# First layer's modulation weights in 256-column pieces, with three pairs of output tiles beside them

## The chip, the cores and the metric

The kernel runs on one core of one Trainium2 chip. The metric is device time in microseconds (us), the median of the runs; before the change it is 2983.74 us (three runs, 2981.06 to 2984.47). Engines are called as the profile calls them: PE (matrix products), PEld (its weight loads), DVE (vector), ACT (scalar), POOL (GpSimd) and SP (which here only issues transfers from HBM).

## The reference

Two transformer blocks run one after the other on 256 tokens of width 2048; everything is float32. The change is in the first layer of the first block, before its attention:

```
silu_c, silu_cc = silu(c), silu(c_ctx)
for l in range(2):
    shift, scale, gate       = split(silu_c  @ w_mod[l] + b_mod[l], 3)     # w_mod[l]: 2048 x 6144
    shift_c, scale_c, gate_c = split(silu_cc @ w_mod[l] + b_mod[l], 3)
    n  = rms_norm(h,  g[l]) * (1 + scale)   + shift        # 256 latent tokens
    nc = rms_norm(hc, g[l]) * (1 + scale_c) + shift_c      # 256 context tokens
    p, pc = split(n @ w_in[l]), split(nc @ w_in[l])        # w_in[l]: 2048 x 7168
    ... four kinds of attention on p, pc; gate; @ w_out[l]; rms_norm; residual ...
```

The second block (a state-space mixer, a latent attention and a feed-forward part) is not touched.

## The kernel before

Activations lie transposed: 16 chunks of 128 features by 512 tokens (256 latent, 256 context). `hb` holds the input, `nH` and `nL` the normed input as a high and a low part, so that three matmuls in a reduced format make one float32 product. Weights of w_in come as a stream of units: one unit is four chunks by 256 output columns, 512 KB, in one of three tiles `raw` (class `Stream`, `RB = 3`). ACT casts a unit to `wh`, DVE subtracts to get `wl`, and only that subtraction frees the `raw` tile for the load of the unit three places later. `W.take` emits cast and subtraction; `W.load_to` emits loads. All instructions are emitted in a fixed order by hand: each engine runs its own in the order in which the code emits them, and SP's loads too, so a load that waits for a tile holds back every load behind it.

The start of layer 0 works like this. `first_norm` squares and sums `hb`, makes the reciprocal root `rb` and multiplies chunks of `hb` by it (`times_rb`, four chunks at a time). Meanwhile `mod_load` brings w_mod in pieces of 512 columns (16 chunks of 256 KB) into 22 slots of 256 KB, and `mod_first` multiplies a piece by silu(c) on PE: four blocks of four matmuls (L706), each of the four on 32 of PE's columns, all in float32. The result is copied out by ACT (`row`), transposed by four tiny matmuls (L717, tile X) and added to the bias (L718). Pieces 4 to 7 are the scale, 0 to 3 the shift; once both pieces for four chunks are there, `gains` makes the factor `gsc`, `norm_in` norms four chunks, and the products of the first two output pairs (`DUO`, the value columns of head group A) over these four chunks run between the blocks of the next two pieces (`first_steps`). The last four chunks of DUO run after the last piece. Then `layer_in` takes one output pair after another, four units each: first the key columns `("k","A",0)`, then the query columns `("q","A",0)`, and so on. Beside each step of `layer_in` run steps of the gate's w_mod pieces and of layer 1's (`mod_later`).

A value pair's products are matmuls with 256 moving columns (L370 to L372), those of the other pairs have 512 (L464 to L466).

Of the kernel before, what the change touches and what calls it, by code (L numbers as in the profile page):

```python
# [19 lines left out]
D = 2048  # L20
# [11 lines left out]
def _r(a, b):  # L32
    return np.arange(a, b)
# [179 lines left out]
def _layout(i):  # L213
    g = {}
    x, ctx = i["x"][0], i["ctx"][0]
    g["xc"] = np.concatenate([_xt(x), _xt(ctx)], axis=2)
    g["cT"] = np.ascontiguousarray(np.stack([i["c"][0].reshape(16, 128).T, i["c_ctx"].reshape(16, 128).T], axis=2))
    for l in range(2):
        units = []
        for key, cols in WIN:  # L220
            units += _pack(i["w_in"][l], 4, cols)
        g[f"win{l}"] = np.concatenate(units)
        g[f"wmod{l}"] = np.concatenate([u for q in range(12) for u in _pack(i["w_mod"][l], 1, _r(512 * q, 512 * q + 512))])
        g[f"wout{l}"] = np.concatenate([u for q in range(8) for u in _pack(i["w_out"][l], 4, _r(256 * q, 256 * q + 256))])
# [20 lines left out]
def program(ctx: ExitStack, tc: tile.TileContext, A, stop=None):  # L245
# [368 lines left out]


    FULL, LATC, CTXC = (0, 512), (0, 256), (256, 512)
    DUO, TRIO = ORDER[0][:2], ORDER[1][:3]
    for l in range(2):
        for part in ("c", "")[1 - l:]:
            for j in range(4):  # L620
                for i in (DUO, TRIO)[l]:
                    W.add((l, *part) + WIN[i][0], f"win{l}", 4 * i + j, 1)
        for i in ORDER[l][3 if l else 2:]:
            W.add((l,) + WIN[i][0], f"win{l}", 4 * i, 4)
        for m in range(8 if l else 5):
# [36 lines left out]
    V.memset(csq, 0.0)  # L662
    V.tensor_copy(out=csq[:, :, 0:2], in_=cs)

    def mod_acc(acc, v, k, w, first):
        if first:
            V.tensor_scalar(acc, w, cs[:, k, v:v + 1], None, op0=MUL)
        else:
            V.scalar_tensor_tensor(out=acc, in0=w, scalar=cs[:, k, v:v + 1], in1=acc, op0=MUL, op1=ADD)  # L669

    def mod_src(l, q, k, n):
        off = (q * 16 + k) * 65536
        return A[f"wmod{l}"][off:off + n * 65536].rearrange("(k p m) -> p k m", p=128, k=n)

    def slots():
# [5 lines left out]

    slot = slots()

    def mod_load(q):

        out = [next(slot) for _ in range(16)]
        k = 0
        while k < 16:
            t, j = out[k]
            n = 1  # L690
            while k + n < 16 and n < 4 and out[k + n][0] is t:
                n += 1
            SY.dma_start(out=t[:, j:j + n, :], in_=mod_src(0, q, k, n))
            k += n
        return [t[:, j, :] for t, j in out]

    fins = []

    def mod_first(q, steps):

        raw = mod_load(q)
        ps = ps_("S")
        for k0 in range(0, 16, 4):

            for j in range(4):
                T.matmul(ps[32 * j:32 * j + 32, :], csq[:, k0 + j, :], raw[k0 + j], start=(k0 == 0), stop=(k0 == 12))  # L706
            if k0 == 0 and fins:
                fins.pop(0)()
            for _ in range(2 if k0 == 0 else 4):
                next(steps, None)  # L710
        row = aw.tile([128, 512], F32, tag=("sqa", "ptl")[q // 4], name="row", bufs=1)
        S.copy(out=row, in_=ps)

        def finish():
            pt = ps_("X")
            for j in range(4):
                T.matmul(pt[:, 2 * j:2 * j + 2], row[:, j * 128:(j + 1) * 128], sel, start=True, stop=True)  # L717
            V.tensor_tensor(out=mod[0][:, :, 4 * q:4 * q + 4].rearrange("p v j -> p j v"),  # L718
                            in0=pt[:, :8].rearrange("p (j v) -> p j v", v=2),
                            in1=bmod[:, 0, 4 * q:4 * q + 4].unsqueeze(2).to_broadcast([128, 4, 2]), op=ADD)  # L720
            if q < 4:
                gains(0, 4 * q, 4 * q + 4)
        fins.append(finish)

    def mod_later(l, q, vs):
# [56 lines left out]
                         scale=gsc[:, v, k:k + 1], bias=mod[0][:, v, k:k + 1])  # L782
        split(nH[:, k, :], nL[:, k, :], t)

    duo_ps = [[ps_(t) for t in tags] for tags in (("mm", "mm"), ("mm", "PT"))]

    def times_rb(j, eng):
        for k in range(4 * j, 4 * j + 4):
            eng.tensor_tensor(out=hb[:, k, 2:514], in0=hb[:, k, 2:514], in1=rb, op=MUL)

    def prod_of(i):
        return products_v if WIN[i][0][0] == "v" else products

    def first_steps(j):

        ws = []
        for i in DUO:
            ws.append(W.take((0,) + WIN[i][0], 256, False))
            yield
        for k in range(4):  # L800
            norm_in(4 * j + k)
            yield
        if j < 3:
            times_rb(j + 1, V)
        for i in range(4):
            for ps, w, prods in zip(duo_ps, ws, map(prod_of, DUO)):
                prods(ps, w[i:i + 1], N_, (FULL, FULL), 4 * j + i, KC, lambda t, k: t[:, k, :])
                for _ in range(2):
                    yield

    for k in range(4):
        SY.dma_start(out=hb[:, 4 * k:4 * k + 4, 2:514], in_=A["xc"][:, 4 * k:4 * k + 4, :])
# [2 lines left out]
    def first_norm():  # L815
# [10 lines left out]
                yield  # L826
        V.tensor_tensor(out=xacc, in0=xacc, in1=xacc2, op=ADD)
        yield
        yield from rstd_row("O", [xacc], 512, D, rb)
        yield  # L830
        times_rb(0, V)

    steps = first_norm()
    for _ in range(4):
        next(steps)
    mod_first(4, steps)
    mod_first(0, steps)
    run_now(steps)
    W.load_to(2)
    for j in range(3):  # L840
        steps = first_steps(j)
        mod_first(5 + j, steps)
        mod_first(1 + j, steps)
        run_now(steps)
        W.load_to(2 * j + 4)
    fins.pop(0)()
    run_now(first_steps(3))

    def dump_split(h, lo, dst):
        o = t2k("dbg")  # L850
        V.tensor_tensor(out=o[:, :h.shape[1]], in0=h.bitcast(F32), in1=lo.bitcast(F32), op=ADD)
# [2 lines left out]
    if stop == "n0":  # L854
# [1 line left out]
            dump_split(nH[:, k, :], nL[:, k, :], A["dbg"][:, k, :])  # L856
        b1.close()
        return


    lamc = const.tile([128, 2, 2], F32, name="lamc")
    lamt, pr = p2k("lamt"), p2k("lamp")
    lamt = lamt.rearrange("p (l i d) -> p l i d", l=2, i=4)
    pr = pr[:, :256].rearrange("p (l i d) -> p l i d", l=2, i=2)
    S.dma_start(out=lamt, in_=A["lam"])
    V.tensor_tensor(out=pr, in0=lamt[:, :, 0::2, :], in1=lamt[:, :, 1::2, :], op=MUL)
    sm4 = small("lam4", 4, 1)
    sm4v = sm4.rearrange("p (l i) -> p l i", i=2)
    V.tensor_reduce(out=sm4v, in_=pr, axis=AX.X, op=ADD)
    S.activation(out=sm4, in_=sm4, func=AF.Exp)  # L870
    for l in range(2):
        li = 0.8 - 0.6 * math.exp(-0.3 * l)

        V.tensor_tensor(out=lamc[:, l, 0:1], in0=sm4v[:, l, 1:2], in1=sm4v[:, l, 0:1], op=SUB)
        V.tensor_scalar(lamc[:, l, 0:1], lamc[:, l, 0:1], li, None, op0=SUB)

        V.tensor_scalar(lamc[:, l, 1:2], subg[:, l:l + 1], 0.5 * (1.0 - li), None, op0=MUL)


    def horner(q, x, cs_, first):  # L880
# [543 lines left out]
        return lambda ps: evac_qk(l, key[0], key[1], key[2], ps, rg[0], n, new)  # L1424

    def layer_in(l):
        for i in ORDER[l][3 if l else 2:]:
            key = WIN[i][0]
            rg = FULL if l == 0 or key[0] in "kv" else LATC
            if l:  # L1430
                beside["rate"] = RATE["long"] if rg == FULL else RATE["short"]
            pair((l,) + key, rg, in_evac(l, key, rg), prods=prod_of(i))

    def layer_in3(part, rg, before, new):

        keys = [WIN[i][0] for i in TRIO]
        trio([(1, *part) + key for key in keys], rg, [in_evac(1, key, rg, new) for key in keys], before, [prod_of(i) for i in TRIO])

    tails = []
    accs, acc_of = (lambda: p2k("zacc"), lambda: acc272[:, 16:]), [None]  # L1440
# [101 lines left out]
        vp.add(mod_later(1, q, (0, 1)))  # L1542
    for q in range(8, 12):
        vp.add(mod_later(1, q, (0,)))
    for i, ps in zip(DUO, duo_ps):
        pend.append(lambda ps=ps, f=in_evac(0, WIN[i][0], FULL): f(ps))
    layer_in(0)
    if stop == "att0":
        drain(pipe, vp)
# [770 lines left out]
```

## Time and profile before

| what | value |
|---|---|
| median of 3 runs | 2983.74 us |
| profiled execution | 2980.39 us, span 2978.6 us |
| PE busy | 2798.6 us, 94% |
| DVE, ACT, POOL busy | 66%, 43%, 18% |
| HBM traffic in the first 117 us | about 387 GB/s in almost every slice |
| HBM traffic over the span | mean 162 GB/s |

The profile is one execution. A busy PE may still be waiting inside a pipelined matmul, so rates are read from the starts of neighbouring instructions. The stretch that the change touches is the first 165 us: up to 117 us transfers run at an even rate, after that PE is nearly always busy.

### The profile page before, as it was taken

The numbers are of one execution on the slowest core, as the hardware profiler recorded it, in microseconds if no ns is written. First come the engines' busy times: TensorE is split into PE (matmuls) and PEld (weight loads), VectorE is DVE, ScalarE is ACT, GpSimd is POOL, SyncE is SP. The second block draws the span as 40 slices with busy tenths as digits, with TensorE's granted clock in tenths as the row PEclk, the third lists the DMA queues.
The fourth block names the chain that finished last, engine by engine and source line by source line (L and its number), as shares of the span: only waits on it lengthen the run. The fifth ranks groups of instructions, "written<-read, shape, count | busy, mean of one in ns | idle before, by whom it ended". The sixth has DMA issues, their size and how long they took to land. (4 is left out here: it accounts for less than half of the span.)

```text
span 2978.6 us, 48955 instructions
## 1 busy us (share of the span) xinstructions
PE 2798.6 (94%) x19022; PEld 2530.3 (85%) x19022; DVE 1980.7 (66%) x3709; ACT 1279.2 (43%) x2196; POOL 526.1 (18%) x501
## 2 busy tenths in 40 slices
PE   6999999998999978999998988899999999999998
PEld 2677878887777978899898987866899999999998
DVE  2377667676676588766676887876865555455544
ACT  2444434244442445534345544234354444344443
POOL 0001100001111161100001125655431110011100
PEclk9999999998999989999999999898999999999999
DMA  9754454543446645534433564432455655666554
GB/s 364 259 163 134 120 150 147 171 130 119 121 139 187 220 155 192 174 100 147 141 125 115 161 191 144 132 110 84 144 160 183 183 183 180 186 187 183 182 176 156
DMA packets 176441, 483.97 MB, mean 162 GB/s; under 512 B 20944, under 2 KB 32848, under 8 KB 176208
## 3 DMA queue, kind: packets, MB, share of 16 engines
q1 hardware_dynamic: 171312, 468.62, 50.2%
q0 software_dynamic: 2880, 9.96, 0.9%
q8 instruction: 149, 2.44, 0.3%
q10 hardware_dynamic: 2016, 2.25, 0.2%
q14 instruction: 84, 0.69, 0.1%
HBM read 468.71 MB, written 12.06 MB: 161 GB/s over the span
## 5 line engine op out<-in xcount | busy, mean ns | idle before, releaser
L327 DVE TENSOR_TENSOR wl<-raw,wh 128x1024 fp32r<-128x1024 f32 (+2 forms) x650 | 809.3, 1250 | 440.5 <-ACT wh L313 435.9
L313 ACT CAST wh<-raw 128x1024 fp32r<-128x1024 f32 (+2 forms) x650 | 669.7, 1036 | 918.1 <-PE mm L465 557.1
L464 PE MATMUL mm<-nH,wh 128*128 128x512 f32 (+1 forms) x2048 | 705.5, 344 | 10.6 <-ACT kp L1109 6.7
L465 PE MATMUL mm<-nL,wh 128*128 128x512 f32 (+1 forms) x2048 | 698.0, 341 | 4.5 <-DVE nL L1097 4.5
L466 PE MATMUL mm<-nH,wl 128*128 128x512 f32 (+1 forms) x2048 | 697.0, 340 | 3.2 <-DVE wl L327 3.1
L464 PEld LDWEIGHTS mm<-nH,wh 128*128 128x128 f32 x2048 | 390.5, 191 | 62.0 <-ACT kp L1109 7.1
L465 PEld LDWEIGHTS mm<-nL,wh 128*128 128x128 f32 x2048 | 390.5, 191 | 50.8 <-DVE nL L1097 6.3
L466 PEld LDWEIGHTS mm<-nH,wl 128*128 128x128 f32 x2048 | 389.8, 190 | 50.7 <-DVE wl L327 4.0
L464 PE MATMUL mm<-ZA,wh 128*128 128x258 f32 (+1 forms) x1408 | 400.4, 284 | 5.0 <-DVE oa L1898 5.0
L466 PE MATMUL mm<-ZA,wl 128*128 128x258 f32 (+1 forms) x1408 | 399.8, 284 | 0.0
L465 PE MATMUL mm<-ZB,wh 128*128 128x258 f32 (+1 forms) x1290 | 363.8, 282 | 0.0
L669 DVE SCALAR_TENSOR_TENSOR acc<-mraw,cs,acc 128x512 f32<-128x512 f32 x420 | 295.6, 754 | 45.8 <-DMA mraw<-in_wmod 43.8
L464 PEld LDWEIGHTS mm<-ZA,wh 128*128 128x128 f32 x1408 | 267.4, 190 | 5.2 <-issue 5.2
L466 PEld LDWEIGHTS mm<-ZA,wl 128*128 128x128 f32 x1408 | 267.4, 190 | 0.0
L465 PEld LDWEIGHTS mm<-ZB,wh 128*128 128x128 f32 x1290 | 245.2, 190 | 0.0
L370 PE MATMUL mm<-wh,nH 128*128 128x256 f32 x736 | 212.5, 289 | 6.7 <-ACT nH L1533 3.4
L372 PE MATMUL mm<-wh,nL 128*128 128x256 f32 x736 | 211.0, 287 | 1.6 <-DVE nL L1535 1.5
L371 PE MATMUL mm<-wl,nH 128*128 128x256 f32 x736 | 210.2, 286 | 0.0
L464 PE MATMUL mm<-yH,wh 128*128 128x256 f32 x688 | 193.5, 281 | 0.0
L465 PE MATMUL mm<-yL,wh 128*128 128x256 f32 x688 | 193.5, 281 | 0.0
L466 PE MATMUL mm<-yH,wl 128*128 128x256 f32 x688 | 193.5, 281 | 0.0
L2258 POOL TENSOR_TENSOR v<-v,a 128x256 f32<-128x256 f32 x43 | 59.4, 1381 | 562.8 <-ACT a L2257 549.6
(499 smaller groups left out, 4885.9 us busy)
## 6 DMA issues: line engine op xcount, KB each, us to landing
raw<-in_win SPq DMA_DIRECT2D x266, 512.0 KB, 3.8
raw<-in_wup SPq DMA_DIRECT2D x172, 512.0 KB, 3.7
mraw<-in_wmod SPq DMA_DIRECT2D x288, 256.0 KB, 2.8
raw<-in_wout SPq DMA_DIRECT2D x76, 512.0 KB, 3.9
raw<-in_wda SPq DMA_DIRECT2D x40, 512.0 KB, 3.7
raw<-in_wdb SPq DMA_DIRECT2D x40, 512.0 KB, 4.2
mraw<-in_wmod SPq DMA_DIRECT2D x28, 512.0 KB, 8.1
mraw<-in_wmod SPq DMA_DIRECT2D x10, 1024.0 KB, 11.1
```

What stands on the lines that cost most here:

```text
L313: S.copy(out=h[:, :size], in_=self.raw[j][:, :size])
L327: V.tensor_sub(lo[:, :size], r[:, :size], h[:, :size].bitcast(F32))
L370: T.matmul(o, ah, w[i][0], start=(k == 0 and t % 2 == 0), stop=False)
L371: T.matmul(o, ah, w[i][1], start=False, stop=False)
L372: T.matmul(o, al, w[i][0], start=False, stop=(k == nk - 1 and t % 2 == 1 and last and i == len(w) - 1))
L464: T.matmul(out, wh, ah, start=start, stop=False)
L465: T.matmul(out, wh, al, start=False, stop=False)
L466: T.matmul(out, wl, ah, start=False, stop=stop)
L669: V.scalar_tensor_tensor(out=acc, in0=w, scalar=cs[:, k, v:v + 1], in1=acc, op0=MUL, op1=ADD)
L2258: P.tensor_tensor(out=v, in0=v, in1=a, op=MUL)
```

## The change

w_mod's columns for scale and shift of layer 0 are laid out anew (`wmodf`) in 16 pieces of 256 columns: scale of chunks 0 and 1, shift of chunks 0 and 1, scale of chunks 2 and 3, and so on. A piece is eight units of 256 KB with two chunks each. `mod_first` now has blocks of 4 matmuls with 256 columns and puts them into tile O, of which there is one, instead of S, of which there are two. Work goes in rounds i = 1 to 8: pieces 2i and 2i+1, the norm of chunks 2i-2 and 2i-1 between them, and six groups of products over chunks 2i-4 and 2i-3, of now three output pairs (the key pair joins, in the two S tiles). A group is one chunk of one pair. Chunks 14 and 15 follow when `layer_in` is due, and each pair is evacuated as it ends. All 16 multiplications by `rb` are emitted at once. The small computation of `lamc` moves from behind this stage to its beginning.

```diff
-    DUO, TRIO = ORDER[0][:2], ORDER[1][:3]
+    TRIO = [o[:3] for o in ORDER]
...
+    lamc = const.tile([128, 2, 2], F32, name="lamc")
+    lamt, pr = p2k("lamt"), p2k("lamp")
...
+    S.dma_start(out=lamt, in_=A["lam"])
+    V.tensor_tensor(out=pr, in0=lamt[:, :, 0::2, :], in1=lamt[:, :, 1::2, :], op=MUL)
...
+    V.tensor_reduce(out=sm4v, in_=pr, axis=AX.X, op=ADD)
+    S.activation(out=sm4, in_=sm4, func=AF.Exp)
...
-    def mod_first(q, steps):
+    def mod_first(h, steps):
...
-        raw = mod_load(q)
-        ps = ps_("S")
+        raw = mod_load(h)
+        ps = ps_("O")[:, :256]
...
-            for _ in range(2 if k0 == 0 else 4):
+            if k0:
                 next(steps, None)
...
+    def norm_steps(i):
+
+        for k in (2 * i, 2 * i + 1):
+            norm_in(k)
+
+    held = []
+
+    def take_first():
+        key = (0,) + WIN[TRIO[0][len(held) % 3]][0]
+        held.append(W.take(key, 256, False))
+
+    def first_steps(i):
+
+        for p, t in enumerate(TRIO[0]):
+            w = held[3 * (i // 2) + p]
+            for c in range(2):
+                prod_of(t)(first_ps[p], w[2 * (i % 2) + c:2 * (i % 2) + c + 1], N_, (FULL, FULL), 2 * i + c, KC, lambda t, k: t[:, k, :])
+                yield
+            if i == 7:
+                in_evac(0, WIN[t][0], FULL)(first_ps[p])
+            elif i % 2:
+
+                take_first()
+        W.load_to(W.low_n + W.RB)
...
-        times_rb(0, V)
+        yield from rstd_row("PT", [xacc], 512, D, rb)
+        for k in range(16):
+            V.tensor_tensor(out=hb[:, k, 2:514], in0=hb[:, k, 2:514], in1=rb, op=MUL)
...
-    mod_first(4, steps)
     mod_first(0, steps)
+    mod_first(1, steps)
     run_now(steps)
-    W.load_to(2)
-    for j in range(3):
-        steps = first_steps(j)
-        mod_first(5 + j, steps)
-        mod_first(1 + j, steps)
+    W.load_to(3)
+    first_ps = [[ps_(t) for t in tags] for tags in (("mm", "mm"), ("mm", "PT"), ("S", "S"))]
+    none = iter(())
+    for i in range(1, 9):
+
+        steps = first_steps(i - 2) if i > 1 else none
+        if i < 8:
+            mod_first(2 * i, steps)
+        else:
+            fins.pop(0)()
+        norm_steps(i - 1)
+        if i == 1:
+            for _ in range(3):
+                take_first()
+            W.load_to(W.low_n + W.RB)
+        if i < 8:
+            mod_first(2 * i + 1, steps)
         run_now(steps)
-        W.load_to(2 * j + 4)
```

First place: DVE at the start, from the root of the norm (`rv`) to the first factors `gsc`. `hb` is the input that is multiplied by `rb`. Before:

```order
L578 TENSOR_SCALAR rv<-O 128x4 [waits PE_49]
L789 TENSOR_TENSOR hb<-hb,rb 128x512 [waits DMAHW3_49,Activation_49]
L789 TENSOR_TENSOR hb<-hb,rb 128x512 x3
L718 TENSOR_TENSOR mod_88<-X,bmod 128x4x2 [waits DMAHW2_49,PE_49]
L718 TENSOR_TENSOR mod_88<-X,bmod 128x4x2 [waits PE_49]
L774 SCALAR_TENSOR_TENSOR gsc<-mod_88,preg 128x2x4 [waits DMAHW4_49,DVE_49]
```

Now:

```order
L580 TENSOR_SCALAR rv<-PT 128x4 [waits PE_49]
L741 TENSOR_TENSOR mod_88<-X,bmod 128x2x2 [waits DMAHW2_49,PE_49]
L856 TENSOR_TENSOR hb<-hb,rb 128x512 [waits DMAHW3_49,Activation_49]
L856 TENSOR_TENSOR hb<-hb,rb 128x512 x3
L856 TENSOR_TENSOR hb<-hb,rb 128x512 [waits DMAHW2_49]
L856 TENSOR_TENSOR hb<-hb,rb 128x512 x3
L856 TENSOR_TENSOR hb<-hb,rb 128x512 [waits DMAHW6_49]
L856 TENSOR_TENSOR hb<-hb,rb 128x512 x3
L856 TENSOR_TENSOR hb<-hb,rb 128x512 [waits DMAHW0_49]
L856 TENSOR_TENSOR hb<-hb,rb 128x512 x3
L741 TENSOR_TENSOR mod_88<-X,bmod 128x2x2 [waits PE_49]
L797 SCALAR_TENSOR_TENSOR gsc<-mod_88,preg 128x2x2 [waits DMAHW4_49,DVE_49]
```

Sixteen multiplications instead of four stand ahead of the first `gsc`.

Second place: SP's loads. Before, around the first pair of w_in loads that waits for DVE (`raw<-in_win`, L297; the others are w_mod):

```order
L693 DMA mraw<-in_wmod 128x512 [waits DMAHW4_49,PE_49]
L297 DMA raw<-in_win 128x1024 [waits DMAHW5_49]
L297 DMA raw<-in_win 128x1024 [waits DMAHW6_49,DVE_49]
L693 DMA mraw<-in_wmod 128x512 [waits DMAHW7_49,PE_49]
L693 DMA mraw<-in_wmod 128x512 [waits DMAHW0_49,PE_49]
```

Now, the last load of piece 2, three loads of w_in, and the loads of piece 3:

```order
L715 DMA mraw<-in_wmodf 128x2x512 [waits DMAHW0_49,PE_49]
L299 DMA raw<-in_win 128x1024 [waits DMAHW1_49,DVE_49]
L299 DMA raw<-in_win 128x1024 [waits DMAHW2_49,DVE_49]
L299 DMA raw<-in_win 128x1024 [waits DMAHW3_49,DVE_49]
L715 DMA mraw<-in_wmodf 128x2x512 [waits DMAHW4_49,PE_49]
L715 DMA mraw<-in_wmodf 128x2x512 [waits DMAHW5_49,PE_49]
```

The same three loads of w_in with a wait for DVE stand ahead of piece 8 and ahead of piece 12.

Third place: ACT in round 3. `wh<-raw` is the cast of a unit, `row<-O` the copy of a piece's result. Now, where before the two casts of a round stood together ahead of its norm:

```order
L734 COPY row<-O 128x256 [waits PE_49]
L315 CAST wh<-raw 128x1024 [waits DMAHW1_49]
L734 COPY row<-O 128x256 [waits PE_49]
L804 ACTIVATE nrm<-hb,mod_88,gsc 128x256 [waits DVE_49]
L804 ACTIVATE nrm<-hb,mod_88,gsc 128x256
L472 CAST nH<-nrm 128x512 [waits Activation_49]
L804 ACTIVATE nrm<-hb,mod_88,gsc 128x256 x2
L472 CAST nH<-nrm 128x512 [waits Activation_49]
L315 CAST wh<-raw 128x1024 [waits DMAHW2_49]
L734 COPY row<-O 128x256 [waits PE_49]
L315 CAST wh<-raw 128x1024 [waits DMAHW3_49]
```

Before, from one result copy to the next norm:

```order
L712 COPY row<-S 128x512 [waits PE_49] x2
L313 CAST wh<-raw 128x1024 [waits DMAHW5_49]
L313 CAST wh<-raw 128x1024 [waits DMAHW6_49]
L781 ACTIVATE nrm<-hb,mod_88,gsc 128x256 [waits DVE_49]
L781 ACTIVATE nrm<-hb,mod_88,gsc 128x256
```

The three casts are now spread over the round, the third behind the result copy of the round's second piece.

## Rows read from the trace of the kernel before

**Rows 1.** The page: granted clock of TensorE in 40 slices of the span.

```profile
PEclk9999999998999989999999999898999999999999
```

**Rows 2.** DMA view, 0 to 160 us: GB/s in 40 slices of 4 us; then issues.

```profile
GB/s 100 244 373 389 387 387 387 387 387 392 396 387 387 385 382 391 398 382 388 388 387 384 401 388 387 385 385 388 399 67 0 253 75 0 0 77 317 209 124 232
...
q10 hardware_dynamic: 1728, 1.20, 2.5%
...
nam<-in_na ACTq DMA_DIRECT2D x1, 128.0 KB, 7.8
```

**Rows 3.** Waits of SP's queue, 0 to 160 us: total us, times, longest.

```profile
SPq L297 <- DVE wl L327: 29.6, 7, 16.4
```

**Rows 4.** Timeline of ACT: start us, us, engine, line, operation, count.

```profile
9.80 0.23 ACT L657 ACTIVATE th<-cT 128x32 f32<-128x32 f32 x1
...
19.39 2.19 ACT L823 ACTIVATE sq<-hb 128x512 f32<-128x512 f32 x4 [0.54 <-DMA hb<-in_xc]
...
132.61 0.21 ACT L870 ACTIVATE lam<-lam 128x4 f32<-128x4 f32 x1 [2.99 <-DVE lam L869]
```

**Rows 5.** Timeline of DVE: the norm's sums, the first multiplications by rb, lam.

```profile
20.06 2.50 DVE L824 TENSOR_TENSOR xacc<-xacc,sq 128x512 f32<-128x512 f32 x4 [0.23 <-ACT sq L823]
22.59 0.69 DVE L827 TENSOR_TENSOR xacc<-xacc,xacc 128x512 f32<-128x512 f32 x1
...
28.13 2.50 DVE L789 TENSOR_TENSOR hb<-hb,rb 128x512 f32<-128x512 f32 x4 [2.97 <-ACT rb L585]
...
131.70 0.43 DVE L866 TENSOR_TENSOR lamp<-lamt 128x256 f32<-128x256 f32 x1 [1.35 <-DMA lamt<-in_lam]
```

**Rows 6.** Timeline of ACT and of DVE: casts, norm and subtractions.

```profile
42.61 2.01 ACT L313 CAST wh<-raw 128x1024 fp32r<-128x1024 f32 x2
51.77 1.09 ACT L781 ACTIVATE nrm<-hb,mod,gsc 128x256 f32<-128x256 f32 x2 [7.15 <-DVE gsc L774]
...
53.42 1.09 ACT L781 ACTIVATE nrm<-hb,mod,gsc 128x256 f32<-128x256 f32 x2
...
51.61 2.36 DVE L327 TENSOR_TENSOR wl<-raw,wh 128x1024 fp32r<-128x1024 f32 x2
```

**Rows 7.** The page: issues of w_in, count, KB each, median us to landing.

```profile
raw<-in_win SPq DMA_DIRECT2D x266, 512.0 KB, 3.8
```

**Rows 8.** Timeline of PE: a block, 24 products, a block, tile X, the next product.

```profile
57.83 1.06 PE L706 MATMUL S<-mraw,csq 128*32 128x512 f32 x8
58.83 0.39 PE L370 MATMUL mm<-wh,nH 128*128 128x256 f32 x1
...
61.89 1.07 PE L706 MATMUL S<-mraw,csq 128*32 128x512 f32 x8
62.89 1.05 PE L717 MATMUL X<-sel,row 128*128 128x2 f32 x8
63.80 0.37 PE L370 MATMUL mm<-wh,nH 128*128 128x256 f32 x1
```

**Rows 9.** Timeline of PE's weight loads: two halves of one block.

```profile
72.55 0.13 PEld L706 LDWEIGHTS S<-mraw,csq 128*32 128x32 f32 x4 [0.30 <-issue]
72.98 0.13 PEld L706 LDWEIGHTS S<-mraw,csq 128*32 128x32 f32 x4 [0.30 <-issue]
```

**Rows 10.** Windows: length, busy PE, PEld, DVE, ACT, POOL, clock, DMA, GB/s.

```profile
120.00:124.00 4.00, 1.50 (x16) 0.97 (x8) 1.70 (x4) 3.43 (x5) 0.00 (x0) 0.85 0.00 0
...
124.70:129.70 5.00, 4.96 (x22) 4.74 (x23) 2.14 (x5) 4.82 (x9) 0.00 (x0) 0.50 0.62 206
...
132.00:136.00 4.00, 4.00 (x35) 4.00 (x35) 1.20 (x8) 0.21 (x1) 0.00 (x0) 1.00 0.00 0
```

**Rows 11.** Timeline of PE and ACT: end of the key pair, start of the query pair.

```profile
163.83 0.40 PE L464 MATMUL mm<-nH,wh 128*128 128x512 f32 x1
...
164.03 0.37 ACT L1139 COPY qf<-mm 128x256 f32<-128x256 f32 x1 [2.44 <-PE mm L466]
...
167.46 1.05 ACT L313 CAST wh<-raw 128x1024 fp32r<-128x1024 f32 x1
```

**Rows 12.** Timeline of SP: the w_in loads behind the last piece.

```profile
104.65 43.99 SPq L297 DMA_DIRECT2D raw<-in_win  x9
```

More of the change, by code (lines that the diff above doesn't have):

```diff
@@ L222, in _layout @@
         g[f"win{l}"] = np.concatenate(units)
-        g[f"wmod{l}"] = np.concatenate([u for q in range(12) for u in _pack(i["w_mod"][l], 1, _r(512 * q, 512 * q + 512))])
+        g[f"wmod{l}"] = np.concatenate([u for q in range(0 if l else 8, 12) for u in _pack(i["w_mod"][l], 1, _r(512 * q, 512 * q + 512))])
         g[f"wout{l}"] = np.concatenate([u for q in range(8) for u in _pack(i["w_out"][l], 4, _r(256 * q, 256 * q + 256))])
+    g["wmodf"] = np.concatenate([u for h in range(8) for c in (2048, 0) for u in _pack(i["w_mod"][0], 2, _r(c + 256 * h, c + 256 * h + 256))])
     g["bmod"] = _cols(i["b_mod"])
@@ L620, in program @@
             for j in range(4):
-                for i in (DUO, TRIO)[l]:
+                for i in TRIO[l]:
                     W.add((l, *part) + WIN[i][0], f"win{l}", 4 * i + j, 1)
-        for i in ORDER[l][3 if l else 2:]:
+        for i in ORDER[l][3:]:
             W.add((l,) + WIN[i][0], f"win{l}", 4 * i, 4)
@@ L663, in program @@
     V.tensor_copy(out=csq[:, :, 0:2], in_=cs)
+    lamc = const.tile([128, 2, 2], F32, name="lamc")
+    lamt, pr = p2k("lamt"), p2k("lamp")
+    lamt = lamt.rearrange("p (l i d) -> p l i d", l=2, i=4)
+    pr = pr[:, :256].rearrange("p (l i d) -> p l i d", l=2, i=2)
+    S.dma_start(out=lamt, in_=A["lam"])
+    V.tensor_tensor(out=pr, in0=lamt[:, :, 0::2, :], in1=lamt[:, :, 1::2, :], op=MUL)
+    sm4 = small("lam4", 4, 1)
+    sm4v = sm4.rearrange("p (l i) -> p l i", i=2)
+    V.tensor_reduce(out=sm4v, in_=pr, axis=AX.X, op=ADD)
+    S.activation(out=sm4, in_=sm4, func=AF.Exp)
+    for l in range(2):
+        li = 0.8 - 0.6 * math.exp(-0.3 * l)
+        V.tensor_tensor(out=lamc[:, l, 0:1], in0=sm4v[:, l, 1:2], in1=sm4v[:, l, 0:1], op=SUB)
+        V.tensor_scalar(lamc[:, l, 0:1], lamc[:, l, 0:1], li, None, op0=SUB)
+        V.tensor_scalar(lamc[:, l, 1:2], subg[:, l:l + 1], 0.5 * (1.0 - li), None, op0=MUL)
     def mod_acc(acc, v, k, w, first):
@@ L671, in mod_src @@
     def mod_src(l, q, k, n):
-        off = (q * 16 + k) * 65536
+        off = ((q if l else q - 8) * 16 + k) * 65536
         return A[f"wmod{l}"][off:off + n * 65536].rearrange("(k p m) -> p k m", p=128, k=n)
@@ L682, in program, with mod_load @@
     slot = slots()
[L684 to L689, printed above, removed]
+    def mod_load(h):
+        out = [next(slot) for _ in range(8)]
+        u = 0
+        while u < 8:
+            t, j = out[u]
             n = 1
-            while k + n < 16 and n < 4 and out[k + n][0] is t:
+            while u + n < 8 and n < 4 and out[u + n][0] is t:
                 n += 1
-            SY.dma_start(out=t[:, j:j + n, :], in_=mod_src(0, q, k, n))
-            k += n
-        return [t[:, j, :] for t, j in out]
+            off = (8 * h + u) * 65536
+            SY.dma_start(out=t[:, j:j + n, :], in_=A["wmodf"][off:off + n * 65536].rearrange("(u p m) -> p u m", p=128, u=n))
+            u += n
+        return [t[:, j, 256 * i:256 * i + 256] for t, j in out for i in range(2)]
     fins = []
-    def mod_first(q, steps):
-        raw = mod_load(q)
-        ps = ps_("S")
+    def mod_first(h, steps):
+        raw = mod_load(h)
+        ps = ps_("O")[:, :256]
         for k0 in range(0, 16, 4):
@@ L708, in mod_first @@
                 fins.pop(0)()
-            for _ in range(2 if k0 == 0 else 4):
+            if k0:
                 next(steps, None)
-        row = aw.tile([128, 512], F32, tag=("sqa", "ptl")[q // 4], name="row", bufs=1)
+        row = aw.tile([128, 512], F32, tag=("sqa", "ptl")[h % 2], name="row", bufs=1)[:, :256]
         S.copy(out=row, in_=ps)
@@ L715, in finish @@
             pt = ps_("X")
-            for j in range(4):
+            for j in range(2):
                 T.matmul(pt[:, 2 * j:2 * j + 2], row[:, j * 128:(j + 1) * 128], sel, start=True, stop=True)
[L718 to L722, printed above, removed]
+            c = h - h % 2 + (h + 1) % 2 * 16
+            V.tensor_tensor(out=mod[0][:, :, c:c + 2].rearrange("p v j -> p j v"),
+                            in0=pt[:, :4].rearrange("p (j v) -> p j v", v=2),
+                            in1=bmod[:, 0, c:c + 2].unsqueeze(2).to_broadcast([128, 2, 2]), op=ADD)
+            if h % 2:
+                gains(0, c, c + 2)
         fins.append(finish)
@@ L783, in norm_in @@
         split(nH[:, k, :], nL[:, k, :], t)
[L785 to L789, printed above, removed]
     def prod_of(i):
         return products_v if WIN[i][0][0] == "v" else products
[L794 to L809, printed above, removed]
+    def norm_steps(i):
[16 more added lines that the diff above has]
+        W.load_to(W.low_n + W.RB)
     for k in range(4):
@@ L828, in first_norm @@
         yield
-        yield from rstd_row("O", [xacc], 512, D, rb)
-        yield
-        times_rb(0, V)
+        yield from rstd_row("PT", [xacc], 512, D, rb)
+        for k in range(16):
+            V.tensor_tensor(out=hb[:, k, 2:514], in0=hb[:, k, 2:514], in1=rb, op=MUL)
+            if k % 4 == 3:
+                yield
     steps = first_norm()
@@ L835, in program @@
         next(steps)
-    mod_first(4, steps)
     mod_first(0, steps)
+    mod_first(1, steps)
     run_now(steps)
-    W.load_to(2)
-    for j in range(3):
-        steps = first_steps(j)
-        mod_first(5 + j, steps)
-        mod_first(1 + j, steps)
+    W.load_to(3)
[14 more added lines that the diff above has]
+            mod_first(2 * i + 1, steps)
         run_now(steps)
-        W.load_to(2 * j + 4)
-    fins.pop(0)()
-    run_now(first_steps(3))
     def dump_split(h, lo, dst):
@@ L858, in program @@
         return
[L861 to L877, printed above, removed]
     def horner(q, x, cs_, first):
@@ L1426, in layer_in @@
     def layer_in(l):
-        for i in ORDER[l][3 if l else 2:]:
+        for i in ORDER[l][3:]:
             key = WIN[i][0]
@@ L1434, in layer_in3 @@
     def layer_in3(part, rg, before, new):
-        keys = [WIN[i][0] for i in TRIO]
-        trio([(1, *part) + key for key in keys], rg, [in_evac(1, key, rg, new) for key in keys], before, [prod_of(i) for i in TRIO])
+        keys = [WIN[i][0] for i in TRIO[1]]
+        trio([(1, *part) + key for key in keys], rg, [in_evac(1, key, rg, new) for key in keys], before, [prod_of(i) for i in TRIO[1]])
     tails = []
@@ L1544, in program @@
         vp.add(mod_later(1, q, (0,)))
-    for i, ps in zip(DUO, duo_ps):
-        pend.append(lambda ps=ps, f=in_evac(0, WIN[i][0], FULL): f(ps))
+    run_now(first_steps(7))
     layer_in(0)
```

## The prediction

> **What bounds the kernel now.** I read the DMA view first. From 12 to 116 us every slice of 4 us carries about 387 GB/s [rows 2]: the start is bound by transfers, 33.5 MB of them w_mod. Then I read PE's timeline. What ends this stage for the rest of the kernel is the first product of the query pair, at 163.8 us [rows 11]; from there the order of work is the same before and after, so I carry the difference at that point to the end. Between 117 and 163.8 us PE does the last four chunks of the two value pairs and the whole key pair: that is what the change moves under the transfers. Over the span the clock is nearly always at its upper level [rows 1]; near this stage it is not (below).
>
> **The change, part by part.** Call the 16 pieces 0 to 15, the rounds 1 to 8, and a product group 12 short matmuls (or 6 long ones).
>
> *Start.* ACT now issues the lamt transfer right after `th`, at 10.0 us [rows 4], and its Exp stands ahead of the squares. The last transfer that ACT issued in the saturated stretch took 7.8 us [rows 2], so I put the landing at 18 us (bounds 12.7, from its 2.7 us alone, an idle queue, and 20). From lamp's start to the end of Exp it is 132.82 - 131.70 = 1.1 us [rows 4, 5]: ACT is free at 19.1. Three squares of 0.55 us, then 14 additions at 2.50/4 = 0.625 us, then the last sum of 0.69 end at 30.2 us; before, 23.3 [rows 4, 5]. That is 6.9 us late (bounds 1.6 and 9), and the first multiplication by rb moves from 28.1 to 35.0.
>
> *Sixteen multiplications.* They take 16 x 0.625 = 10.0 us in place of 2.5 [rows 5] and stand ahead of gsc: 45.0, with bias and gsc 45.3.
>
> *The first loads held back.* Behind gsc, ACT norms two chunks (1.65 us each by the starts 51.77 and 53.42) and casts three units (1.0 each); DVE's subtractions of 1.18 end at 50.8, 52.0 and 53.2 [rows 6]. Only these free the three raw tiles, and SP's three loads of w_in stand ahead of piece 3. What was issued by then is 1.2 MB of constants, 4.2 of hb, 6.3 of pieces 0 to 2 and 1.6 of w_in, 13.3 MB; at 387 GB/s, with 4.6 us for the first three slices [rows 2], it has landed at 39 us. So the queue is empty from 39 to 51 us. In the kernel before, SP's loads waited 29.6 us for such subtractions too, but the longest wait, 16.4 us, lies in the nine loads behind the last piece, where no w_mod was queued behind them [rows 3, 12].
>
> The third load lands 3.8 us after its issue [rows 7], at 57.0; piece 3 (2.1 MB, 5.4 us) at 62.4, and the second load of piece 4 at 66.5. PE has nothing but four blocks until then.
>
> [...]
>
> *A round on PE.* A group of 12 products takes 1.44 us: 24 products and one block lie between the starts 57.83 and 61.89, 4.06 us, of which the block is 1.18 [rows 8]. In a block the two halves start 0.43 us apart [rows 9], so 0.85 us are columns and 0.33 fixed; with 256 columns I take 0.43 + 0.33 = 0.76 us (bounds: half of it all, 0.59, and no saving, 1.18). Tile X cost 0.91 us for eight records [rows 8], now 0.46 for four. A piece is 4 x 0.76 + 0.46 + 3 x 1.44 = 7.8 us, a round 15.6. Its transfers (4.2 MB of w_mod and 0.8 of w_in on average) need 12.9: PE, not the queue, is the limit of a round.
>
> *Loads held back again.* Ahead of pieces 8 and 12 stand three loads of w_in whose last waits for a subtraction that comes behind the copy of the round's second piece. That copy can start one group before the round's end: 0.5 copy + 1.05 cast + 1.2 subtraction less 1.44 is 1.4 us past the end. Then 3.8 us for the load, and 1.35 us for the first two units of piece 8 (2.7 for the first four of piece 12): PE stands 6.6 and 7.9 us.
>
> *Clock.* After 2.5 us without matmuls the granted clock was 0.50 (1.2 GHz) for 5 us, with 22 records done in 5.0 us where full clock did 35 in 4.0 [rows 10]: 2.5 us lost. I charge that at four restarts (rounds 2, 4, 6 and the query pair); bounds 0 and 5 us each.
>
> The Trainium skill ("TensorE: Matmul & The Clock Gate", section on HAM oscillation) warns against this shape of loop: where PE waits for a transfer before every group of matmuls, each group starts at the half clock. It agrees with the 0.50 in [rows 10]. Charged at four restarts the sum is 10 us higher than without it; a loop that waits at every piece is the fourth rival.
>
> *The end of the stage.* After piece 15 come X (0.5) and twelve groups, 17.3 us; the last norm lies beside the first six. Then ACT first copies the key pair out, 167.46 - 164.03 = 3.4 us before its next cast [rows 11], and nothing covers that now: with the cast and the semaphores 4.8 us. Before, the same copies lay beside the query pair. The four turns of later modulation work that lay beside the key pair move one pair back, where PE is the bound: nothing (bounds 0 and 2).
>
> *Sum.* Round 2 from 66.5: three blocks, three groups (6.6), piece 5 (7.8) and 2.5 of clock: 83.4. Round 3: 99.0. Wait 6.6: 105.6. Round 4 with clock 18.1: 123.7. Round 5: 139.3. Wait 7.9: 147.2. Round 6: 165.3. Round 7: 180.9. Tail 17.8: 198.7. Evacuation 4.8 and clock 2.5: 206.0, against 163.8. That is 42.2 us later: 2980.4 becomes 3022.6 in the profiled execution, which lies 3.3 us under the median; on the median it is 2983.7 + 42.2 = 3026 us.
>
> **Rivals.**
> 1. *The queue never runs dry and PE keeps up* (faster). All bytes up to piece 15 (45.2 MB) land at 121 us; with the tail of 17.8 and 7.3 behind it the query pair starts at 147: 17 us gained, 2967 us. It speaks for this that before the queue was full throughout [rows 2]. Against it: SP's order, and that it needs rounds of 13 us on PE, under 0.5 us a block. With my blocks, and still no dry queue, it would be 41 + 6 x 15.6 + 17.8 + 7.3 = 160, 4 us gained: 2980, the same.
> 2. *A milder start.* lamt lands early (5 us less), blocks cost 0.59 us (48 in rounds 2 to 7: 8 less), no loss by clock (10 less): 3003 us.
> 3. *Blocks do not shrink*, 1.18 us each: 48 x 0.42 = 20 us more, 3046.
> 4. *PE stays at 1.2 GHz*, because it waits at nearly every piece. A round's columns double, some 12 us each, 74 less the 7.5 charged already: 3092. Against it: in rounds 2 to 7 the pieces of a round but the first lie ready, since PE is slower than the queue.
>
> **Chances.** My forecast 76%, with a range of its own from 3008 to 3044; rival 1 3%, and 3% for its slower form with no change; rival 2 9%; rival 3 6%; rival 4 3%. About 0.2%, 6 us, is what a measurement of this kernel can tell from no change. Faster 4%, same 4%, slower 92%. The range for 8 in 10: from 3002, where the milder start ends, to 3046, where blocks that do not shrink do.
>
> **What would show it.** In the profile after: traffic near zero from about 39 to 51 us, and again around the ends of rounds 3 and 5 (near 100 and 140 us); SP's w_in loads waiting for DVE wl in the middle of the w_mod loads; sixteen multiplications by rb in a row from 35 us; PE idle until 58 us but for the blocks of pieces 0 to 2, then clock 0.50 after each wait; the query pair's first product near 206 us. The prediction is wrong if traffic is even up to 121 us, if a block of 256 columns costs under 0.5 us or over 1 us, or if the query pair starts before 170 us.

## The result and the profile after

The changed kernel takes 3026.31 us (median of 4 runs, 3023.15 to 3035.87), the kernel before 2984.1 us (4 runs, 2981.06 to 2985.93): a ratio of 1.0148, 95% interval 1.0124 to 1.0172, 42.2 us more. The profiled execution took 3026.79 us with a span of 3025.0, 46.4 more than before's span.

The DMA view of the kernel after, 0 to 240 us, here in 40 slices of 6 us (answers to [rows 2]):

```profile
GB/s 198 256 384 386 389 400 204 0 1 260 384 386 387 385 211 90 42 180 325 394 382 253 90 82 181 392 385 387 153 85 87 90 0 0 0 265 194 237 197 72
```

The even rate of [rows 2] is gone. There is a hole from about 40 to 53 us, and two dips, near 96 and near 138 us. The timeline of SP's queue in the same stretch shows why (start, us from the first to the last of the group, count), with the queue's waits above it (total us, times, longest; answers to [rows 3]):

```profile
SPq L299 <- DVE wl L329: 105.7, 17, 21.9
```

```profile
23.05 10.59 SPq L715 DMA_DIRECT2D mraw<-in_wmodf  x7
53.46 2.60 SPq L299 DMA_DIRECT2D raw<-in_win  x3
56.15 25.43 SPq L715 DMA_DIRECT2D mraw<-in_wmodf  x22
90.35 14.22 SPq L299 DMA_DIRECT2D raw<-in_win  x3
105.08 18.93 SPq L715 DMA_DIRECT2D mraw<-in_wmodf  x19
131.53 14.20 SPq L299 DMA_DIRECT2D raw<-in_win  x3
```

Three times a group of w_in loads that waits for DVE's subtraction `wl` stands ahead of w_mod loads: from 33.64 to 53.46 us SP issues nothing; near 90 and 131 us the three loads are spread over 14 us. Of the 105.7 us of waiting, 62.5 lie at these three places; the rest, the longest single wait of 21.9 us included, lies behind the last piece, as in the kernel before [rows 12]. DVE's timeline gives the chain that ends in that first subtraction (answers to [rows 5, 6]):

```profile
16.87 0.42 DVE L673 TENSOR_TENSOR lamp<-lamt 128x256 f32<-128x256 f32 x1 [5.74 <-DMA lamt<-in_lam]
...
28.13 0.69 DVE L852 TENSOR_TENSOR xacc<-xacc,xacc 128x512 f32<-128x512 f32 x1
...
37.94 9.72 DVE L856 TENSOR_TENSOR hb<-hb,rb 128x512 f32<-128x512 f32 x16 [3.47 <-ACT rb L587]
...
47.65 0.15 DVE L797 SCALAR_TENSOR_TENSOR gsc<-mod,preg 128x4 f32<-128x4 f32 x1
...
52.20 3.50 DVE L329 TENSOR_TENSOR wl<-raw,wh 128x1024 fp32r<-128x1024 f32 x3 [0.26 <-ACT wh L315]
```

PE's timeline shows the waits for the late pieces (in brackets: idle before, and what ended it) and the regular rounds between them (answers to [rows 8, 11]):

```profile
62.91 1.08 PE L728 MATMUL O<-mraw,csq 128*32 128x256 f32 x8 [20.66 <-DMA mraw<-in_wmodf]
...
71.97 0.58 PE L372 MATMUL mm<-wh,nH 128*128 128x256 f32 x1
...
83.40 0.64 PE L728 MATMUL O<-mraw,csq 128*32 128x256 f32 x8
...
85.57 0.64 PE L728 MATMUL O<-mraw,csq 128*32 128x256 f32 x8
...
87.75 0.64 PE L728 MATMUL O<-mraw,csq 128*32 128x256 f32 x8
88.31 0.61 PE L739 MATMUL X<-sel,row 128*128 128x2 f32 x4
...
109.14 1.81 PE L728 MATMUL O<-mraw,csq 128*32 128x256 f32 x8 [5.99 <-DMA mraw<-in_wmodf]
...
152.21 1.08 PE L728 MATMUL O<-mraw,csq 128*32 128x256 f32 x8 [7.88 <-DMA mraw<-in_wmodf]
...
207.93 0.79 PE L466 MATMUL mm<-nH,wh 128*128 128x512 f32 x1 [4.55 <-ACT wh L315]
```

The query pair's first product comes at 207.93 us against 163.83 [rows 11]: 44.1 us late. The last wait ahead of it is the key pair's copies on ACT, from 202.71 us on, with the casts that PE needs queued behind them:

```profile
202.71 0.37 ACT L1155 COPY qf<-S 128x256 f32<-128x256 f32 x1 [1.51 <-PE S L468]
...
206.83 2.94 ACT L315 CAST wh<-raw 128x1024 fp32r<-128x1024 f32 x3
...
233.40 0.37 ACT L1155 COPY qf<-mm 128x256 f32<-128x256 f32 x1 [2.44 <-PE mm L468]
```

The last row is the query pair's last product copied out. In before the same copy (L1139) starts at

```profile
186.52 0.37 ACT L1139 COPY qf<-mm 128x256 f32<-128x256 f32 x1 [2.44 <-PE mm L466]
```

so the stage ends 46.9 us later. The span grew by 46.4, but the difference does not run unchanged from here to the end. The first norm of the second layer on ACT starts, in before and in after, at

```profile
1083.18 1.73 ACT L1533 ACTIVATE nH<-nrm,mod 128x256 fp32r<-128x256 f32 x4
```

```profile
1126.02 1.73 ACT L1549 ACTIVATE nH<-nrm,mod 128x256 fp32r<-128x256 f32 x4
```

42.8 us apart: the changed kernel gets 4.1 us back behind the stage. Most of that shows where PE waits for the first layer's attention weights (`pth`), in before and in after:

```profile
441.13 0.58 PE L464 MATMUL O<-pth,vh 128*128 128x256 f32 x1 [2.90 <-ACT pth L470]
```

```profile
484.89 0.38 PE L466 MATMUL O<-pth,vh 128*128 128x256 f32 x1 [1.11 <-ACT pth L472]
```

The wait is shorter, and the matmul behind it takes 0.38 in place of 0.58 us. The steps of later modulation work lie elsewhere beside the attention now; that they are the reason was not tried. The other 3.6 us of the 46.4 come in the second block, which the change does not touch. Windows of after (length, busy PE, PEld, DVE, ACT, POOL, granted clock, DMA share, GB/s; answers to [rows 10]) show the clock around the waits:

```profile
48.00:52.00 4.00, 0.00 (x0) 0.00 (x0) 1.38 (x2) 3.94 (x7) 0.00 (x0) 0.50 0.00 2
...
72.00:76.00 4.00, 4.00 (x25) 2.97 (x21) 0.00 (x0) 0.00 (x0) 0.00 (x0) 0.50 1.05 388
76.00:80.00 4.00, 4.00 (x32) 3.42 (x32) 0.00 (x0) 1.37 (x3) 0.00 (x0) 0.89 1.05 387
...
108.00:112.00 4.00, 2.75 (x12) 1.33 (x12) 0.07 (x1) 0.00 (x0) 0.00 (x0) 0.50 0.91 303
```

The clock is at 0.50 after the waits, and in round 2 it stays there long after the matmuls have started again at 62.91 us.

### The profile page after: what moved, and what is told of

Read it like the earlier page. It is cut to its first block, busy times and chain, and to the rows that moved or that the text cites. A ratio compares the mean times of both kernels' runs of the same rounds, so it can differ in the third digit from the quotient of the medians.

```text
span 3025.0 us, 49478 instructions
## 1 busy us (share of the span) xinstructions
PE 2812.7 (93%) x19278; PEld 2542.0 (84%) x19278; DVE 1984.9 (66%) x3721; ACT 1281.1 (42%) x2204; POOL 516.4 (17%) x501
## 5 line engine op out<-in xcount | busy, mean ns | idle before, releaser
L466 PE MATMUL mm<-nH,wh 128*128 128x256 f32 (+1 forms) x2016 | 694.4, 344 | 14.3 <-ACT kp L1125 6.7
L467 PE MATMUL mm<-nL,wh 128*128 128x256 f32 (+1 forms) x2016 | 687.5, 341 | 4.6 <-DVE nL L1113 4.6
L468 PE MATMUL mm<-nH,wl 128*128 128x256 f32 (+1 forms) x2016 | 686.1, 340 | 2.6 <-DVE wl L329 2.6
L372 PEld LDWEIGHTS mm<-wh,nH 128*128 128x128 f32 x736 | 142.6, 194 | 16.3 <-issue 12.2
```

What stands on the lines that cost most here:

```text
L372: T.matmul(o, ah, w[i][0], start=(k == 0 and t % 2 == 0), stop=False)
L466: T.matmul(out, wh, ah, start=start, stop=False)
L467: T.matmul(out, wh, al, start=False, stop=False)
L468: T.matmul(out, wl, ah, start=False, stop=stop)
```

## The experiments

Theory A is the prediction's: w_in loads that wait for `wl` in SP's one queue hold the w_mod loads back, and between these stops PE's rounds set the pace. The rivals that each run could have favoured stand in its expectation. Differences in us are between the medians of a kernel and of the kernel before on the same chip. By their intervals the change itself costs 37 to 51 us; the runs with one small edit each (a shorter start 33 to 44, half as many blocks 27 to 39, casts ahead 29 to 40) overlap with that, so their gains are not shown by medians alone. For them the traces count: the query pair starts 5.8, 9.3 and 7.0 us sooner than in after.

**Loads behind the second piece.** The w_in loads are issued behind the w_mod loads of the round's second piece, so that nothing which waits for `wl` stands ahead of a piece that PE needs sooner:

```diff
@@ first_steps
-        W.load_to(W.low_n + W.RB)
@@ the loop over rounds
-            W.load_to(W.low_n + W.RB)          # after the first three take_first()
         if i < 8:
             mod_first(2 * i + 1, steps)
+        if i % 2 == 0:
+            W.load_to(W.low_n + W.RB)
```

> The changed kernel, but the loads of w_in are emitted once per two rounds behind the w_mod loads of the second piece of an even round, so that none of them stands ahead of a piece that PE needs next. Same work, same transfers. Theory A (the load queue held back by w_in loads that wait for DVE's subtractions): the empty stretch from 40 to 53 us goes, products can begin when the first units are cast and subtracted, near 55 us instead of 72; PE's two waits of 6.0 and 7.9 us go and with them two restarts at half clock; together 30 to 37 us, 2989 to 2996 us. Rival B (PE's own round, with its 64 short blocks between the groups, sets the pace, and the gaps in the queue are only its shadow): no change, 3023 to 3029 us, with PE's rounds still 15.4 us and the first product still near 72 us. Rival C (the half clock alone): the waits stay but shorter, 3012 to 3020 us.

Measured: 2990.83 us (10 runs), ratio 1.0027 (1.0016 to 1.0039): 5.6 us above before in place of 42.2. The DMA view, 0 to 240 us, and PE's first product and the query pair's:

```profile
GB/s 194 298 385 387 392 396 386 385 387 397 384 389 293 229 221 347 392 380 347 188 351 382 111 36 87 90 0 0 27 283 180 245 208 66 175 186 131 168 14 78
```

```profile
57.01 0.58 PE L372 MATMUL mm<-wh,nH 128*128 128x256 f32 x1
...
170.92 0.79 PE L466 MATMUL mm<-nH,wh 128*128 128x512 f32 x1 [4.56 <-ACT wh L315]
```

The rate stays near 387 GB/s to 72 us, the first product comes 15.0 us sooner (57.01 for 71.97), the waits of 5.99 and 7.88 us are gone, and the query pair starts 37.0 us sooner. This edit changes nothing but the order in one queue, so most of the loss is shown to be that order. A round still takes 15.3 us on PE, and 7.1 us stay at the query pair: 3.9 of them go when the start is mended too (third run), 3.2 do not.

**A shorter start.** The lambda block goes back behind the loop, and hb is multiplied by rb two chunks at a time, right before they are needed:

```diff
-        for k in range(16):
-            V.tensor_tensor(out=hb[:, k, 2:514], in0=hb[:, k, 2:514], in1=rb, op=MUL)
+        times_rb(0)                            # two chunks
...
         for k in (2 * i, 2 * i + 1):
             norm_in(k)
+        if i < 7:
+            times_rb(i + 1)
```

> The changed kernel with the start of before: the lamc block behind the stage again, and the multiplications by rb two chunks at a time, each pair a round ahead of its norm, instead of all 16 ahead of the first gsc. The loads stay as in the changed kernel. Theory A: the first gsc comes when piece 1 is through tile X, near 36 us instead of 47.7, the held-back loads of w_in about 12 us earlier (41 instead of 53), and everything behind them too: 3012 to 3017 us, PE's waits at pieces 8 and 12 unchanged at 6 and 8 us. Rival B gives the same or less, since PE would be through pieces 0 to 2 no earlier: 3014 to 3026 us.

Measured: 3020.94 us (4 runs), ratio 1.0129 (1.0112 to 1.0146), 35.7 above before: 6.5 gained where 9 to 14 were expected, a miss. The time lies in rival B's range; but B forecast nothing from the order of loads, and the first run refutes that. DVE, ACT and SP of this run:

```profile
35.88 0.17 DVE L779 SCALAR_TENSOR_TENSOR gsc<-mod,preg 128x4 f32<-128x4 f32 x1
...
46.53 3.49 DVE L329 TENSOR_TENSOR wl<-raw,wh 128x1024 fp32r<-128x1024 f32 x3
```

```profile
41.03 0.37 ACT L716 COPY row<-O 128x256 f32<-128x256 f32 x1 [6.92 <-PE O L710]
41.30 1.09 ACT L786 ACTIVATE nrm<-hb,mod,gsc 128x256 f32<-128x256 f32 x2
```

```profile
47.78 2.60 SPq L299 DMA_DIRECT2D raw<-in_win  x3
```

`gsc` is ready 11.8 us sooner (35.88 for 47.65), as expected, but the norm that uses it stands on ACT behind the copy of piece 2's result, and piece 2 lands only then: ACT idles 6.9 us. The loads resume 5.7 us sooner (47.78 for 53.46), and by that much the query pair comes sooner (202.17 for 207.93). What the block and the multiplications are worth one by one was not tried.

**Both.** The two edits together.

> Both edits: loads of w_in behind, and the start of before. Theory A: products begin near 46 us, six rounds of 15.4 us follow without a wait for transfers, then 17.5 us of tail and 4.6 of uncovered evacuation plus a clock restart: the query pair starts near 163, where it started before (163.8), 2978 to 2988 us, the same as before. So three pairs beside the transfers would by themselves bring nothing, because a round on PE is longer than its transfers. If transfers and not PE set a round once the queue is full (rival D), a round takes 12.9 us and the time is 2962 to 2970 us. Rival B: above 3010 us.

Measured: 2986.09 us (12 runs), ratio 1.0008 (0.9995 to 1.0022), no difference from before. The first product comes at 52.60 us (46 expected) and the query pair starts at 167.00 us (163 expected), 3.2 us behind before. The stage ends 6.2 us behind (the last copy at 192.70 for 186.52); at the second layer's first norm 2.3 are left (1085.49 for 1083.18). The median comes out as before with the help of what the changed kernels get back behind the stage.

**The lambda block in the kernel before.** If the block itself cost the time, moving it to the start of the kernel before must make that slower:

```diff
+    (the block that makes lamc)                # moved here, unchanged
     def mod_acc(acc, v, k, w, first):
...
-    (the block that makes lamc)
```

> The kernel before with one part of the change alone: the lamc block, its transfer included, moved to the beginning. ACT is held up to the landing of lamt near 17 us, and the root of the norm comes 5 to 8 us later (multiplications by rb near 34 to 36 instead of 28). But the first gsc of this kernel waits for pieces that land at 49 us: theory A says no change, 2982 to 2987 us. Rival E (a later start of the norm costs its delay in any kernel): 2989 to 2992 us.

Measured: 2986.9 us (12 runs), ratio 1.0009 (0.9998 to 1.0021), no difference. Its DVE timeline:

```profile
35.13 2.50 DVE L808 TENSOR_TENSOR hb<-hb,rb 128x512 f32<-128x512 f32 x4 [4.33 <-ACT rb L585]
...
51.71 0.17 DVE L793 SCALAR_TENSOR_TENSOR gsc<-mod,preg 128x8 f32<-128x8 f32 x1
```

The multiplication by rb does move, from 28.13 [rows 5] to 35.13 us; but `gsc` waited for w_mod's column pieces anyway. A late start is paid for only where something waits for it, as the w_in loads do after the change.

**Half as many blocks.** Two blocks of four matmuls become one of eight, so that PE changes between blocks and products half as often:

```diff
-        for k0 in range(0, 16, 4):
-            for j in range(4):
-                T.matmul(ps[32 * j:32 * j + 32, :], ..., start=(k0 == 0), stop=(k0 == 12))
+        for k0 in range(0, 16, 8):
+            for j in range(8):
+                T.matmul(ps[32 * (j % 4):32 * (j % 4) + 32, :], ..., start=(k0 + j < 4), stop=(k0 + j >= 12))
```

> The changed kernel with two blocks of a piece put together: eight short matmuls, one group of products, eight short matmuls, two groups. Same matmuls, loads and waits. Theory A: a block costs 0.43 us of columns and 0.33 us for the change of kind, so a piece is 0.66 us shorter: 12 pieces of rounds 2 to 7 make 8 us, a round takes 14.0 instead of 15.4 us, 3016 to 3020 us. Rival F (the 0.33 us is not a cost of the change but of the matmuls, so it does not go): no change, 3024 to 3028 us.

Measured: 3016.75 us (6 runs), ratio 1.011 (1.0089 to 1.0131), 31.2 above before: 11.0 gained. Every second of PE's blocks, in rounds without a wait:

```profile
80.21 1.07 PE L728 MATMUL O<-mraw,csq 128*32 128x256 f32 x16
...
87.30 1.07 PE L728 MATMUL O<-mraw,csq 128*32 128x256 f32 x16
...
94.45 1.07 PE L728 MATMUL O<-mraw,csq 128*32 128x256 f32 x16
```

A piece now takes 7.1 us, where a round of two takes 15.4 in after, 7.7 each. Two blocks fewer save some 0.6 us a piece, 7 us in twelve pieces: the fixed part of a block is real.

**Casts ahead of the key pair's copies.** In the last round ACT casts the query pair's first two units before it copies the key pair out:

```diff
             if i == 7:
+                if p == 2:
+                    W.low_to(W.used + 2)
                 in_evac(0, WIN[t][0], FULL)(first_ps[p])
```

> The changed kernel with casts and subtractions of the query pair's first two units emitted ahead of the key pair's evacuation. Theory A: the 4.6 us in which PE waits for ACT's ten copies and a cast go, and with them the restart at half clock (2 to 3 us): the query pair starts within 1 us of the last group, 3018 to 3022 us. Rival G (the copies that come later then hold up the query pair's own evacuation, its norm or the heads): the gap goes but the time stays, 3025 us.

Measured: 3019.47 us (4 runs), ratio 1.0114 (1.0096 to 1.0133), 33.9 above before: 8.3 gained. The key pair's last and the query pair's first product on PE:

```profile
200.74 0.40 PE L468 MATMUL S<-nH,wl 128*128 128x512 f32 x1
200.98 0.40 PE L466 MATMUL mm<-nH,wh 128*128 128x512 f32 x1
```

They are 0.24 us apart instead of 4.95 (202.98 to 207.93 in after), and the granted clock stays at 1.00. In the trace that is 7.5 us, 4.7 of the wait and 2.8 of clock (below). The key pair itself ends 2.2 us sooner in this execution (200.74 for 202.98); the edit does not reach that.

**All four edits.**

> Loads behind, the start of before, merged blocks and early casts together. Theory A adds the single terms to the 2986 us of the first two: 8 us for the blocks, 5 to 7 for the evacuation: 2969 to 2975 us, which is below both kernels; the query pair's first product near 153 us. Rival D2 (with a round of 14.0 us the transfers of 12.9 us and their waits set the pace): 2976 to 2981 us, with waits of PE for w_mod in the rounds.

Measured: 2971.28 us (9 runs) against 2985.56 (14 runs), ratio 0.9956 (0.9941 to 0.997): faster than both kernels, by 0.4% on before and clear of no change. Its DMA view over 0 to 240 us, PE at the query pair and ACT at its end:

```profile
GB/s 191 295 386 387 393 395 385 386 387 398 387 387 385 400 387 386 370 359 284 389 184 87 87 134 0 0 183 257 168 234 181 164 218 131 133 41 77 61 175 119
```

```profile
154.93 0.39 PE L466 MATMUL mm<-nH,wh 128*128 128x512 f32 x1
```

```profile
177.61 0.37 ACT L1162 COPY qf<-mm 128x256 f32<-128x256 f32 x1 [2.44 <-PE mm L468]
```

The rate is even to 96 us, and the query pair starts 8.9 us ahead of before. The medians differ by 14.3 (9.0 to 17.6 by the interval). Of the other 5, 3.3 come behind the stage, as after gets its 4.1 back: the second layer's first norm starts at 1070.95 us, 12.2 ahead of before.

**The first norm sooner.** On top of that, `norm_steps(0)` and the first three casts stand ahead of the copy on which the second run was stuck:

```diff
     none = iter(())
+    fins.pop(0)()
+    norm_steps(0)
+    for _ in range(3):
+        take_first()
...
-        norm_steps(i - 1)
+        if i > 1:
+            norm_steps(i - 1)
```

> The one before, and in addition the first norm and the first three casts stand ahead of piece 2's result copy on ACT, where they waited for piece 2 to land. Theory A: the first subtraction ends near 40 us instead of 48, products begin when pieces 2 to 4 are in, near 47 us instead of 52.6, and PE runs on from there: 3 to 6 us less than the kernel with the four edits. If transfers set the pace by then (rival D2): no change against it.

Measured: 2971.63 us (5 runs), ratio 0.9954 (0.9938 to 0.997), no difference from the run above. DVE's subtraction and PE's block of piece 4 here, and that block with the four edits alone:

```profile
41.02 3.49 DVE L329 TENSOR_TENSOR wl<-raw,wh 128x1024 fp32r<-128x1024 f32 x3
```

```profile
49.72 1.08 PE L710 MATMUL O<-mraw,csq 128*32 128x256 f32 x8 [1.07 <-DMA mraw<-in_wmodf]
```

```profile
49.58 1.08 PE L710 MATMUL O<-mraw,csq 128*32 128x256 f32 x8 [0.83 <-DMA mraw<-in_wmodf]
```

The subtraction comes 5.3 us sooner (41.02 for 46.35), and the piece no sooner: with the queue full, transfers set the pace up to there, and what frees a tile sooner buys nothing. Theory A's 3 to 6 us did not come; the rival, that transfers set the pace by then, forecast no change.

## Why the prediction was right, point by point

The direction, the mechanism and the size held: 3026 predicted, 3026.31 measured. The runs show the main cause by taking it away (37.0 of the 44.1 us at the query pair go with the order of loads). The closeness of the median is luck: two errors cancel. At the stage's end the loss is 46.9 us where the sum had 42.2. The prediction then carried the difference unchanged to the end, because the order of work is the same from there; but 4.1 us come back between the stage and the second layer, where 42.8 is left. Two other changed kernels do the like: the one with both start and order mended gets 3.9 back, the one with all four edits 3.3. Step by step, with the trace of after:

| step | predicted | measured |
|---|---|---|
| lamp starts | 18 us | 16.87 |
| last sum ends | 30.2 | 28.8 |
| first multiplication by rb | 35.0 | 37.94 |
| sixteen multiplications | 10.0 long | 9.72 |
| first three wl end | 53.2 | 55.7 |
| queue empty | 39 to 51 | 40 to 53 |
| second part of piece 4 | 66.5 | 70.96 |
| round 2 ends | 83.4 | 87.75 |
| rounds 3, 5, 7 | 15.6 each | 15.4, 15.4, 15.2 |
| waits for pieces 8 and 12 | 6.6 and 7.9 | 5.99 and 7.88 |
| rounds 4 and 6, with clock | 18.1 each | 19.8 and 18.2 |
| evacuation of the key pair | 4.8 | 4.55 |

*From the last sum to rb* is the step that missed most. The sum took this stretch over from before (4.85 us); it took 9.1. In PE's order three blocks and an X of the pieces stand between its two small products here:

```profile
28.88 1.87 PE L574 MATMUL PT<-ones,xacc 128*128 128x1 f32 x8 [3.90 <-DVE xacc L852]
30.67 1.08 PE L728 MATMUL O<-mraw,csq 128*32 128x256 f32 x8
...
35.21 2.08 PE L585 MATMUL PT<-ident,rr 128*128 128x128 f32 x8
```

These and a wait fill 4.5 us, and the small products take 1.87 and 2.08 us; in before they took 1.05 and 1.16 with one block between. The durations are those that PE shows elsewhere at a granted clock of 0.50 (a block 1.08, an X 1.01, in place of 0.64 and 0.61), while the block of 512 columns in before takes 1.07 there, as in [rows 8]: the sum charged no slow clock in this place. The earlier sum gave back 1.4 us, so rb was 2.9 us late. SP resumed 2.5 us late by it (53.46 for 51); the other 2.0 of the 4.5 by which piece 4 was late lie in the transfers behind the hole.

*The block.* 0.76 us for a block of 256 columns, halfway by [rows 9], was right: 83.40 to 85.57 us is a block and a group, 2.17 us, and without the group of 1.44 it is 0.73. "Blocks do not shrink" (a period of 2.62) and the "milder start" (2.03) both fall with it; merging the blocks confirmed the fixed part.

*The clock* was charged 2.5 us at each restart. Round 6 took 2.8 more than round 5, round 4 4.4 more than round 3, and the query pair's own stretch is 25.5 us (207.93 to 233.40) against 22.7, 2.8 more. Of round 4's 4.4 us 1.1 are transfers: its first block takes 1.81 in place of 1.08 us, with a wait for w_mod inside it, and PE waits another 0.39 at 112.28. So piece 8 cost 7.1 us of waiting and not 5.99, and the clock 3.3. (The sum's 1.4 us past the end of a round is 1.3 by its own terms.) "PE stays at 1.2 GHz" is wrong: the rounds without a wait ran at full rate. The Trainium skill ("TensorE: Matmul & The Clock Gate", section on HAM oscillation) lets each group that follows a wait for a transfer start at the half clock. The trace agrees at the three long waits, ahead of pieces 3, 8 and 12: X takes 1.01, 1.01 and 1.02 us there, and the block 1.08 at pieces 3 and 12, against 0.61 and 0.64 in the rounds between. Not every wait does it: in the run with all four edits the block behind a wait of 2.16 us for w_mod, at 40.09, takes 0.64, at a granted clock of 1.00.

*The queue that never runs dry* is what the runs with reordered loads built. The prediction gave that case with these blocks the time of before, 2980 on 2983.7; 2986.09 on 2985.27 was measured with both start and order mended, the query pair at 167.00 us for 160; what is won back behind the stage hides that it starts later. Only with fewer changes between blocks and products and with the copies covered did the three pairs beside the transfers gain.

## What to carry to other kernels

A load that waits for a buffer which computed work must free should not stand, in an in-order queue, ahead of loads for which the critical engine waits next: look at every place where the change puts one, and place it behind the loads of the current step. Before more work is laid beside a stream of transfers, add up the engine's round (15.4 us here) and the transfers' (12.9 by the prediction's estimate): the excess is paid in every round, and short blocks that alternate with other products make it grow. When the last pair of a stage ends with nothing beside it, cast the next weights before its results are copied out. And read the difference between two kernels at several places along the run, not at the end alone: here it is 46.9, 42.8 and 46.4 us.

## What the runs showed of the hardware

The granted clock did not come back at once after a long wait. In [rows 10] it was 0.50 for 5 us after 2.5 us without matmuls. Here, after 20.66 us of idle PE, matmuls ran again from 62.91 us, and the window from 72 to 76 us, busy throughout, still has 0.50; 76 to 80 us reads 0.89. In the run with early casts, after 20.00 us of idle PE, blocks take 0.64 again at 68.14 us, 5.6 us after the restart at 62.58. What sets the delay was not tried.

The clock's column and the durations part early in the kernel. The window

```profile
32.00:36.00 4.00, 3.75 (x23) 2.12 (x24) 0.17 (x1) 0.19 (x1) 0.04 (x1) 1.00 1.03 392
```

reads 1.00, but its blocks and X take 1.08 and 1.01 us, as elsewhere at 0.50. Whether the column or the engine is late there stays open; for a sum, the durations count.
